# Norm table sent with x's first tile, five row chunks taken three steps at a time, weight copies inside DRAM begun earlier and at half the rate, sample sums ahead of the last store

## The chip, the cores and the metric

One core of a Trainium2 chip runs the kernel as one program. The metric is the device time of one execution in microseconds (us). The engines are TensorE (PE; its weight loads are listed apart as PEld), VectorE (DVE), ScalarE (ACT), GpSimd (POOL) and SyncE (SP). SP, ACT and POOL issue DMA transfers, all of which are carried by the core's 16 DMA engines.

## The reference

One step of a single decoder layer, in fp32, for 512 prompt tokens and 8 x 8 sample tokens (T = 576 columns in all), with a model width of 2048:

```
h  = rms_norm(x, norm_in)
z  = h @ w_in                      # all projections of both head groups at once
att = top-k sparse attention       # 8 heads of 128; an indexer (16 heads of 64) scores the keys, the best 256
                                   # (128 for the prompt) are kept; samples attend to 1024 paged keys as well
ob  = gated linear attention       # 4 heads, dk 128, dv 256, chunks of 64, a running state S
x  = x + concat(att * silu(ga), rms_norm(ob, gla_norm) * silu(gb)) @ w_out
y  = rms_norm(x, norm_f)           # 512 prompt rows and 64 sample rows
```

New keys, values, indexer keys and the states S are outputs too.

## The kernel before

**Numbers.** Every fp32 operand of a product is split in two rounded parts: a high part (`w_hi`, `xh`: a cast) and the rest (`w_lo`, `xl`: the operand less its high part). A product is then three matmuls, high by high, low by high and high by low. So each weight tile of 128x512 needs a load (`w_raw`, 256 KB, issued by SP), a cast on ACT and a subtraction on DVE, or on POOL during the first four heads (`lo_eng`). `wload` (L184) does these three.

**Stages.** The program is one long row of matmuls, with the work of the other engines laid beside it:
1. 0 to 26 us: `split_x(k)` loads x's 16 tiles of 128x576, multiplies each by its column of the table `gn_in` (norm_in) and splits it; `kmm` (L244) and `kmm_q` (L249) use each tile at once for the first two weight blocks, whose weights `first_piece` (L205) loads in pieces. For tile 0, x comes in two halves and the pieces of the first block are loaded by ACT's queue, as is `gn_in`.
2. to 130 us: the indexer's projections; to about 235 us: the queries and keys of heads 0 and 1, then `vgroup(0)`: values of four heads for all tokens. A value group has five accumulators (four chunks of 128 prompt rows, `ps_g`, and one for the samples, `ps_v`) and runs over 16 steps k, each with a weight of its own. Among its matmuls stand the sample indexer's products (`pq`, L507 and L508) of a page's keys (`kch`, `kcl`, L500 to L504).
3. to about 370 us: scores (`head_scores`, softmax at L732 to L739), gates (`head_g`) and outputs (`head_out`, transposes at L750) of heads 0 to 3, while DVE runs the top-k searches; to 640 us heads 4 to 7 with the samples' paged attention; `vgroup(1)` stands in head 4.
4. to 950 us: the gated linear attention (the state `Sst`, L1227). The value groups 2 and 3 belong to it.
5. to the end: the output product in seven block products (a form with sums of weight blocks), then a residual add, the final norm and the stores.

**Order.** A scheduler places each engine's instructions by estimated times; `tc.high_priority` moves what it holds ahead, `tc.issue_after(x)` puts an instruction behind x. Each engine then runs its own list in order. So an instruction that waits holds up everything behind it on its engine.

**Copies inside DRAM.** The sums of weight blocks for the output product are made by DMA alone: `block_parts` gives 16 parts of 512 KB. Each is first copied inside DRAM (`started`, issued by SP behind a weight load, L191) and later has a second block added to it by an accumulating DMA (`added`, issued by POOL behind a `w_lo`, L200). In the kernel before, the copies begin after `vgroup(0)`, one with each weight load, and the additions begin in head 2, one with each `w_lo` that POOL makes.

**End.** `store(c)` (L1440) scales the four quarters of 128 rows c by their root; of `store(1)`, quarter 3 is on DVE (L1447), quarters 0 and 2 on POOL (L1449), quarter 1 on ACT. The sample rows' last quarter comes from two products of 256 columns (`acc_s`); `sample_sum` adds the parts (L1354), `sample_square` (L1486) squares them, `mean_square`, `root_of` and a reciprocal give the factor, and L1581 to L1585 scale and store `y_smp`.

Of the kernel before, what the change touches and what calls it, by code (L numbers as in the profile page):

```python
# [20 lines left out]
P = 128  # L21
D = 2048
NK = D // P
# [96 lines left out]
def build(tc, I, O):  # L120
# [41 lines left out]

    gn_in = cp.tile([P, NK], F32, name="gn_in")
    eps = cp.tile([P, 1], F32, name="eps")
# [19 lines left out]
    def wload(src, far=0):  # L184
        with tc.high_priority(offset=WOFF):
            raw = wp.tile([P, 512], F32, name="w_raw", tag="w_raw", bufs=3)
            d = sy.dma_start(raw, src)
            wloads.append(d.ins if hasattr(d, "ins") else d)
            if started:
                with tc.issue_after(wloads[-1]):  # L190
                    sy.dma_start(*started.pop(0))  # L191
            hi = wp.tile([P, 512], F32R, name="w_hi", tag="w_hi", bufs=5)
            c = se.copy(hi, raw)  # L193
            rounded.append(getattr(c, "ins", c))
            lo = low_tile(wp, 5, far)
            c = lo_eng[0].tensor_tensor(out=lo, in0=raw, in1=hi.bitcast(F32), op=ALU.subtract)  # L196
# [4 lines left out]
        return hi, lo  # L201

    first_w = {}

# [13 lines left out]
    def split_x(k):  # L218
        xk = p0.tile([P, T], F32, name="xr", bufs=6)
        parts = (slice(HT, T), slice(0, HT)) if k == 0 else (slice(0, T),)  # L220
        for c in parts:
            sy.dma_start(xk[:, c], I["xT"][:, k, c])
        if k == 0:
            first_piece(0, k)
            se.dma_start(gn_in, I["norm_in"])
        if k % 2 == 0:
# [3 lines left out]
        l = xp.tile([P, T], F32R, name="xl", tag="xl")  # L230
        for c in parts:
            se.activation(h[:, c], xk[:, c], AF.Copy, scale=gn_in[:, k : k + 1])  # L232
        for c in parts:
            ve.scalar_tensor_tensor(out=l[:, c], in0=xk[:, c], scalar=gn_in[:, k : k + 1], in1=h[:, c].bitcast(F32), op0=ALU.mult, op1=ALU.subtract)
        xh.append(h)
# [408 lines left out]
    def vgroup(g, step):  # L644
# [19 lines left out]
        for k in range(NK):  # L664
# [106 lines left out]
    def head(h, bg, n):  # L771
# [194 lines left out]
    lo_eng[0] = ve  # L966
    assert not added
    with tc.issue_after(px["end"]):
# [227 lines left out]
    def recur(h, eL, qE, kDt, ks):  # L1196
# [17 lines left out]
        for i in range(4):  # L1214
# [10 lines left out]
            Sn = gl.tile([P, DV], F32, name="Sst", bufs=2)  # L1225
            if S is None:
                ve.tensor_copy(Sn, pU[:, :DV])  # L1227
            else:
                ve.scalar_tensor_tensor(out=Sn, in0=S, scalar=eL[:, i : i + 1], in1=pU[:, :DV], op0=ALU.mult, op1=ALU.add)
            S = Sn  # L1230
# [119 lines left out]
    y_smp = yp_.tile([P, D // 2], F32, name="y_smp")  # L1350
    nfs = yp_.tile([P, 256], F32, name="nfs")

# [56 lines left out]
    for c in range(2):  # L1409
        sy.dma_start(nfs[TS * c : TS * c + TS], I["norm_f"][:, 1024 * c + 768 : 1024 * c + 1024].to_broadcast([TS, 256]))  # L1410

# [27 lines left out]

    def store(c):  # L1440
        root_of(yr[:, c : c + 1], slice(0, P), c)
        ve.reciprocal(out=yr[:, c : c + 1], in_=yr[:, c : c + 1])
        done = {}
        for q in range(4):
            yc = place(c, q)
            if c > 1 or q == 3:
                done[ve] = ve.scalar_tensor_tensor(out=two(yc), in0=two(yc), scalar=yr[:, c : c + 1], in1=nfb(q), op0=ALU.mult, op1=ALU.mult)  # L1447
            elif q == 0 or (c == 1 and q == 2):
# [15 lines left out]

    def sample_sum(acc, q, c0, n, last=None):
        r, r2 = halves_of(q)
        d0 = 512 * q + c0
        yc = y_smp[r, d0 % 1024 : d0 % 1024 + n]
        t = ysm[q][:, c0 : c0 + n]
        if last is not None:  # L1470
            with behind(last, se):
                last[se] = se.copy(yl[r, c0 : c0 + n], acc[r2, :n])
            with behind(last, ve):
                plus(yc, acc[r, :n], t[r])
                last[ve] = plus(yc, yc, yl[r, c0 : c0 + n])
        else:
            plus(yc, acc[r, :n], t[r])
            plus(t[r], acc[r2, :n], t[r2])
            plus(yc, yc, t[r])

    def sample_square(q, c0, n, col):
        r, _ = halves_of(q)
        d0 = 512 * q + c0
        yc = y_smp[r, d0 % 1024 : d0 % 1024 + n]
        jk = ev.tile([P, 512], F32, name="yjk", tag="e1", bufs=2)
        se.activation(jk[r, :n], yc, AF.Square, accum_out=ysq[r, 4, col : col + 1])  # L1486

    def sample_weigh(q, c0, n):
        r, _ = halves_of(q)
        d0 = 512 * q + c0  # L1490
        for j in range(d0, d0 + n, 256):
            if j % 1024 < 768:
                yj = y_smp[r, j % 1024 : j % 1024 + 256]
                plus(yj, yj, a21[r, j // 256, :], ALU.mult)

    def sample_out(acc, q, c0, n, col):
        sample_sum(acc, q, c0, n)
        sample_square(q, c0, n, col)
        sample_weigh(q, c0, n)

# [23 lines left out]
    for p in range(2):  # L1524
# [12 lines left out]
        plus(y11[:, p], y11[:, p], acc)  # L1537
        sample_out(smp, q1, 0, 512, q1)
        for c in (0, 1):
# [4 lines left out]
    plus(y12[:, 0], y12[:, 0], acc)  # L1544
    sample_out(smp, 1, 0, 512, 1)
    for c in (0, 1):
# [3 lines left out]

    yl = ev.tile([P, T], F32, name="yl", tag="e0", bufs=2)[:, :512]
    r, r2 = halves_of(3)
    se.copy(yl[r], ysm[3][r2])
    plus(ysm[3][r], ysm[3][r], yl[r])
    accs = (pg.tile([P, 2, 512], F32, name="acc", tag="ps_g")[:, 0, :], pm.tile([P, 512], F32, name="acc_u", tag="pu", bufs=1))
    smp = [mm1("acc_s") for _ in range(2)]
    halves = (slice(0, 256), slice(256, 512))
    ws = [w for k in range(0, 8, 2) for w in weights("b22", 1, k)]
    for i in range(2):
# [3 lines left out]
        square(i, 3)  # L1563
        last = store(i)
    for s in range(2):
        with tc.issue_after(getattr(end, "ins", end)):
            for k in range(8):
                end = single(smp[s][:, :256], 8 + k, *(w[:, halves[s]] for w in ws[k]), k == 0, k == 7)
        sample_sum(smp[s], 3, 256 * s, 256, last)
        sample_square(3, 256 * s, 256, 3 + s)  # L1570
    with behind(last, ve):
        mean_square(pre[:, 4:5], ysq[:, 4:5, :4])
        ve.tensor_copy(pre[TS:, 5:6], pre[:TS, 4:5])
        last[ve] = ve.scalar_tensor_tensor(out=pre[TS:, 4:5], in0=pre[TS:, 4:5], scalar=-EPS, in1=pre[TS:, 5:6], op0=ALU.add, op1=ALU.add)
    with behind(last, ve):
        sample_weigh(3, 0, 256)
    root_of(yr[TS:, 5:6], slice(TS, P), 4)
    for r in (slice(0, TS), slice(TS, P)):
        ve.reciprocal(out=yr[r, 4:5], in_=yr[TS:, 5:6])
    a, b, c = y_smp[:, :448], y_smp[:, 448:768], y_smp[:, 768:]  # L1580
    se.activation(a, a, AF.Copy, scale=yr[:, 4:5])  # L1581
    se.dma_start(O["ys"][:, :448], a)
    ve.scalar_tensor_tensor(out=c, in0=c, scalar=yr[:, 4:5], in1=nfs, op0=ALU.mult, op1=ALU.mult)
    ve.tensor_scalar(out=b, in0=b, scalar1=yr[:, 4:5], scalar2=None, op0=ALU.mult)
    sy.dma_start(O["ys"][:, 448:], y_smp[:, 448:])  # L1585
    yp_s.close()
# [17 lines left out]
def host_inputs(a):  # L1604
# [4 lines left out]
    page = a["page_table"]  # L1609
    x = np.concatenate([xp, xs], 0)  # L1610
    ins = {
        "xT": c(x.reshape(T, NK, P).transpose(2, 1, 0)),
        "xp": c(xp),
# [50 lines left out]
```

## Time and profile before

| | |
|---|---|
| median of 3 runs | 1196.19 us (1195.59 to 1202.51) |
| the profiled execution's own time | 1196.95 us |
| its span (first to last recorded event) | 1194.9 us |
| PE busy | 1180.9 us, 99% of the span |
| DVE, ACT, POOL busy | 729.8, 585.9, 308.8 us |
| granted TensorE clock | 9 tenths or more in all 40 slices |
| bytes moved by DMA | 259.85 MB, 217 GB/s on average |

The profile is of one execution; 2.05 us of its time lie outside its span. Busy shares are averages over the stages above. Where PE is busy all the time, another engine's work shows in the time only if PE waits for it, or if it lies ahead of the first matmul or behind the last.

### The profile page before, as it was taken

The numbers are of one execution on the slowest core, as the hardware profiler recorded it, in microseconds if no ns is written. First come the engines' busy times: TensorE is split into PE (matmuls) and PEld (weight loads), VectorE is DVE, ScalarE is ACT, GpSimd is POOL, SyncE is SP. The second block draws the span as 40 slices with busy tenths as digits, with TensorE's granted clock in tenths as the row PEclk, the third lists the DMA queues.
The fourth block names the chain that finished last, engine by engine and source line by source line (L and its number), as shares of the span: only waits on it lengthen the run. The fifth ranks groups of instructions, "written<-read, shape, count | busy, mean of one in ns | idle before, by whom it ended". The sixth has DMA issues, their size and how long they took to land.

```text
span 1194.9 us, 23011 instructions
## 1 busy us (share of the span) xinstructions
PE 1180.9 (99%) x8389; PEld 1040.2 (87%) x8389; DVE 729.8 (61%) x1349; ACT 585.9 (49%) x1046; POOL 308.8 (26%) x495
## 2 busy tenths in 40 slices
PE   9999999999999999999999999999999999999997
PEld 8999997899999778889898769778899999888886
DVE  7678899699656433565453724434566444657686
ACT  6887565444443232354342635326367533544454
POOL 1225665546631110000110511321042121012101
PEclk9999999999999999999999999999999999999999
DMA  9562233877973999999667675677715377669873
GB/s 298 205 178 95 91 105 109 277 226 171 218 186 99 354 361 346 326 331 348 214 223 244 222 262 199 222 244 235 250 46 179 123 252 247 214 172 238 243 228 119
DMA packets 142563, 259.85 MB, mean 217 GB/s; under 512 B 15777, under 2 KB 39218, under 8 KB 141874
## 3 DMA queue, kind: packets, MB, share of 16 engines
q1 hardware_dynamic: 136370, 243.73, 60.9%
q0 software_dynamic: 4928, 13.11, 6.2%
q10 hardware_dynamic: 1152, 1.55, 0.4%
q8 instruction: 66, 1.08, 0.4%
q14 instruction: 47, 0.39, 0.1%
HBM read 224.49 MB, written 50.48 MB: 230 GB/s over the span
## 4 chain that ended last, share of the span: by engine, by line
PE 78%; DVE 9%; DMA 6%; issue 3%; ACT 2%; SPq 1%; POOL 0%; ACTq 0%; DVEq 0%; POOLq 0%
PE ps_g L244 35%; PE ps_g L249 6%; PE ps_g L658 4%; PE ps_g L657 4%; PE ps_g L659 4%; PE acc L1379 2%; PE acc L1380 2%; PE acc L1378 2%; PE pS L279 2%; PE pOs L279 2%; DMA y<-in_xp 2%; DVE w_lo L1373 1%; PE ps_v L653 1%; PE ps_v L654 1%; DVE wk L538 1%
## 5 line engine op out<-in xcount | busy, mean ns | idle before, releaser
L244 PE MATMUL ps_g<-xh,w_hi 128*128 128x288 f32 x1312 | 391.1, 298 | 0.8 <-ACT xh L232 0.8
L244 PE MATMUL ps_g<-xl,w_hi 128*128 128x288 f32 x1312 | 287.3, 296 | 0.1
L244 PE MATMUL ps_g<-xh,w_lo 128*128 128x288 f32 x1312 | 286.1, 296 | 0.0
L193 ACT CAST w_hi<-w_raw 128x512 fp32r<-128x512 f32 x252 | 154.4, 619 | 230.2 <-PE ps_g L244 84.0
L244 PEld LDWEIGHTS ps_g<-xh,w_hi 128*128 128x128 f32 x1312 | 246.4, 188 | 4.4 <-issue 1.7
L196 DVE TENSOR_TENSOR w_lo<-w_raw,w_hi 128x512 fp32r<-128x512 f32 x188 | 136.3, 729 | 173.9 <-ACT w_hi L193 167.8
L244 PEld LDWEIGHTS ps_g<-xl,w_hi 128*128 128x128 f32 x1312 | 211.9, 188 | 2.6 <-issue 1.2
L244 PEld LDWEIGHTS ps_g<-xh,w_lo 128*128 128x128 f32 x1312 | 211.8, 188 | 1.0
L657 PE MATMUL ps_g<-w_hi,xh 128*128 128x512 f32 x256 | 101.0, 396 | 0.9 <-DVE ev_t L617 0.9
L196 POOL TENSOR_TENSOR w_lo<-w_raw,w_hi 128x512 fp32r<-128x512 f32 x64 | 86.7, 1356 | 54.8 <-ACT w_hi L193 45.1
L659 PE MATMUL ps_g<-w_hi,xl 128*128 128x512 f32 x256 | 100.4, 392 | 0.0
L658 PE MATMUL ps_g<-w_lo,xh 128*128 128x512 f32 x256 | 100.3, 392 | 0.0
L1373 DVE TENSOR_TENSOR w_lo<-w_raw,w_hi 128x1024 fp32r<-128x1024 f32 (+1 forms) x60 | 68.4, 1150 | 41.8 <-ACT w_hi L1371 41.4
L1371 ACT CAST w_hi<-w_raw 128x1024 fp32r<-128x1024 f32 (+1 forms) x60 | 59.4, 995 | 61.5 <-PE acc_s L1383 21.1
L1379 PE MATMUL acc<-w_lo,fh 128*128 128x512 f32 x216 | 84.0, 389 | 0.0
L1380 PE MATMUL acc<-w_hi,fl 128*128 128x512 f32 x216 | 84.0, 389 | 0.0
L1378 PE MATMUL acc<-w_hi,fh 128*128 128x512 f32 x216 | 83.5, 389 | 0.0
L657 PEld LDWEIGHTS ps_g<-w_hi,xh 128*128 128x128 f32 x256 | 48.0, 188 | 11.2 <-DVE ev_t L617 1.3
L658 PEld LDWEIGHTS ps_g<-w_lo,xh 128*128 128x128 f32 x256 | 48.1, 188 | 10.5 <-issue 0.8
L659 PEld LDWEIGHTS ps_g<-w_hi,xl 128*128 128x128 f32 x256 | 48.1, 188 | 9.9
L668 POOL CAST xs<-xh 128x64 fp32r<-128x64 f32 x64 | 19.8, 309 | 119.5 <-PE ps_v L654 113.8
L618 POOL TENSOR_TENSOR ev_sw<-ev_sw,c_s 128x576 f32<-128x576 f32 x16 | 25.0, 1565 | 95.7 <-ACT ev_sw L615 95.6
(390 smaller groups left out, 2118.3 us busy)
## 6 DMA issues: line engine op xcount, KB each, us to landing
w_raw<-in_w SPq DMA_DIRECT2D x188, 256.0 KB, 3.6
kt<-in_ck SPq DMA_DIRECT2D x128, 256.0 KB, 5.2
vt<-in_cv SPq DMA_DIRECT2D x128, 256.0 KB, 5.2
w_raw<-in_wv SPq DMA_DIRECT2D x64, 256.0 KB, 3.2
w_raw<-st SPq DMA_DIRECT2D x32, 512.0 KB, 4.8
w_raw<-in_wo SPq DMA_DIRECT2D x20, 512.0 KB, 6.7
st<-in_wo SPq DMA_DIRECT2D x16, 512.0 KB, 4.7
bs<-in_wo SPq DMA_DIRECT2D x32, 256.0 KB, 5.3
```

The lines of the kernel that those rows point to most:

```text
L193: c = se.copy(hi, raw)
L196: c = lo_eng[0].tensor_tensor(out=lo, in0=raw, in1=hi.bitcast(F32), op=ALU.subtract)
L244: pe.matmul(ps[:, j, :HT], wt, xt[k][:, j * HT : (j + 1) * HT], start=(k == 0 and n in (0, 2)), stop=(k == NK - 1 and n > 3))
L249: m = pe.matmul(ps[:, 0, :TQ], wt[:, c], xt[:, P:T], start=(k == 0 and n == 0), stop=(k == NK - 1 and n == 2))
L657: pe.matmul(accs[i], xh[k][:, c], wh, start=a, stop=False)
L658: pe.matmul(accs[i], xh[k][:, c], wl, start=False, stop=False)
L659: m = pe.matmul(accs[i], xl[k][:, c], wh, start=False, stop=b)
L1371: se.copy(hi, raw)
L1373: ve.tensor_tensor(out=lo, in0=raw, in1=hi.bitcast(F32), op=ALU.subtract)
L1378: pe.matmul(acc, f[0][:, k, c], wh, start=a, stop=False)
L1379: pe.matmul(acc, f[0][:, k, c], wl, start=False, stop=False)
L1380: return pe.matmul(acc, f[1][:, k, c], wh, start=False, stop=b)
```

## The change

It has five parts.

1. The table `gn_in` becomes the first 16 columns of a tile `x0` that also holds x's tile 0. The first DMA brings the table and the first half (304 columns), the second the other half. ACT's DMA for the table is gone.
2. In `vgroup`, the first three steps k (before: the first two) are taken together, accumulator by accumulator.
3. The copies inside DRAM begin just before `vgroup(0)`, one with every second weight load; the additions begin in head 0, one with every second `w_lo` of POOL.
4. The update of the state `Sst` is placed under a priority (`ahead`).
5. At the end, the mean of the samples' first three quarters is made before the last products; the sums of the first 256 columns of the last quarter come before quarter 3 of `store(1)`; both halves of the last quarter are squared in one instruction of 512; the final scaling is 512 columns on ACT and 512 on DVE (with a table `nfs` of 512 columns that holds norm_f), in place of 448, 256 and 320.

```
-    gn_in = cp.tile([P, NK], F32, name="gn_in")
+    x0 = p0.tile([P, NK + T], F32, name="x0")
+    gn_in = x0[:, :NK]
...
-            if started:
+            if started and len(wloads) % 2:
                 with tc.issue_after(wloads[-1]):
                     sy.dma_start(*started.pop(0))
...
             if lo_eng[0] is po_:
-                if added:
+                turn[0] += 1
+                if added and turn[0] % 2:
                     with tc.issue_after(getattr(c, "ins", c)):
                         po_.dma_start(*added.pop(0), accum_op=ALU.add)
...
         if k == 0:
+            sy.dma_start(x0[:, : NK + HT], I["x0"][:, : NK + HT])
+            sy.dma_start(x0[:, NK + HT :], I["x0"][:, NK + HT :])
             first_piece(0, k)
-            se.dma_start(gn_in, I["norm_in"])
...
-            if k == 1:
+            if k == 2:
                 for i in (0, 1, 4, 2, 3):
-                    for kk in (0, 1):
+                    for kk in range(3):
                         mms(i, kk)
...
-            elif 1 < k < NK - 2:
+            elif 2 < k < NK - 2:
...
+            for to, src, _ in block_parts():
+                started.append((to, src))
             vgroup(0, lambda k: pump(bg, 2) if k % 4 == 3 else None)
...
-            for to, src, _ in block_parts():
-                started.append((to, src))
-        if h == 2:
-            assert not started
             for to, _, more in block_parts():
                 added.append((to, more))
...
+            with ahead():
+                if S is None:
+                    ve.tensor_copy(Sn, pU[:, :DV])
+                else:
+                    ve.scalar_tensor_tensor(out=Sn, in0=S, scalar=eL[:, i : i + 1], in1=pU[:, :DV], op0=ALU.mult, op1=ALU.add)
...
+    mean_square(pre[:, 4:5], ysq[:, 4:5, :3])
...
+        if s == 0:
+            plus(ys, a[r], t[r])
+            plus(t[r], a[r2], t[r2])
+            done[ve] = plus(ys, ys, t[r])
+            done = store(1, done)
+        else:
+            with behind(done, se):
+                se.copy(yl[r], a[r2])
+            with behind(done, ve):
+                plus(ys, a[r], t[r])
+                plus(ys, ys, yl[r])
+    jk = ev.tile([P, 512], F32, name="yjk", tag="e1", bufs=2)
+    se.activation(jk[r], y_smp[r, 512:], AF.Square, accum_out=ysq[r, 4, 4:5])
...
-    ve.scalar_tensor_tensor(out=c, in0=c, scalar=yr[:, 4:5], in1=nfs, op0=ALU.mult, op1=ALU.mult)
-    ve.tensor_scalar(out=b, in0=b, scalar1=yr[:, 4:5], scalar2=None, op0=ALU.mult)
-    sy.dma_start(O["ys"][:, 448:], y_smp[:, 448:])
+    ve.scalar_tensor_tensor(out=c, in0=c, scalar=yr[:, 4:5], in1=nfs, op0=ALU.mult, op1=ALU.mult)
+    sy.dma_start(O["ys"][:, 512:], c)
```

What the scheduler makes of it is read from each engine's list of instructions. First the start, on DVE, from its first cast on. `w_hi` and `w_lo` of 128x256 are pieces of the two first weight blocks, `xl` the low part of x's tile 0 in two halves. Before:

```order
L215 CAST w_hi<-w_raw 128x256
L216 TENSOR_TENSOR w_lo<-w_raw,w_hi 128x256
L234 SCALAR_TENSOR_TENSOR xl<-xr,gn_in,xh 128x288 x2
L215 CAST w_hi<-w_raw 128x256
L216 TENSOR_TENSOR w_lo<-w_raw,w_hi 128x256
```

After (the tile `x0` bears the name x_94 here):

```order
L218 CAST w_hi<-w_raw 128x256
L239 SCALAR_TENSOR_TENSOR xl<-x_94,xh 128x288
L219 TENSOR_TENSOR w_lo<-w_raw,w_hi 128x256
L218 CAST w_hi<-w_raw 128x256
L239 SCALAR_TENSOR_TENSOR xl<-x_94,xh 128x288
L219 TENSOR_TENSOR w_lo<-w_raw,w_hi 128x256
```

The first `w_lo` now stands behind the first `xl`, and `xl` waits for `xh` from ACT.

Second, PE where the last head projection ends and `vgroup(0)` begins, with the tiles' numbers: `pq_2322` and `pq_2441` are the products of two consecutive pages' keys, `ps_g` the row chunks. Before, from the first `pq` on, and then from the second:

```order
L507 MATMUL pq_2322<-kch_2256,qiS_603 128x512
L508 MATMUL pq_2322<-kcl_2259,qiS_603 128x512
L657 MATMUL ps_g_2392<-w_hi_2397,xh_125 128x512
L658 MATMUL ps_g_2392<-w_lo_2399,xh_125 128x512
L659 MATMUL ps_g_2392<-w_hi_2397,xl_126 128x512
...
L653 MATMUL ps_v_2394<-w_hi_2406,xs_2410 128x512
L654 MATMUL ps_v_2394<-w_lo_2408,xs_2410 128x512
L507 MATMUL pq_2441<-kch_2340,qiS_603 128x512
L508 MATMUL pq_2441<-kcl_2343,qiS_603 128x512
```

After, at the same place:

```order
L512 MATMUL pq_2320<-kch_2254,qiS_601 128x512
L513 MATMUL pq_2320<-kcl_2257,qiS_601 128x512
L512 MATMUL pq_2412<-kch_2338,qiS_601 128x512
L513 MATMUL pq_2412<-kcl_2341,qiS_601 128x512
L662 MATMUL ps_g_2390<-w_hi_2396,xh_123 128x512
L663 MATMUL ps_g_2390<-w_lo_2398,xh_123 128x512
L664 MATMUL ps_g_2390<-w_hi_2396,xl_124 128x512
L662 MATMUL ps_g_2390<-w_hi_2405,xh_140 128x512
L663 MATMUL ps_g_2390<-w_lo_2407,xh_140 128x512
L664 MATMUL ps_g_2390<-w_hi_2405,xl_141 128x512
L662 MATMUL ps_g_2390<-w_hi_2448,xh_161 128x512
```

The second page's product has moved 16 matmuls forward, directly behind the first, and the third step's weight is used by the seventh matmul of the group. In the value groups 1 and 2, PE's list has not changed at all, and in group 3 only at one place.

Third, DVE at the very end, from the last add of a row chunk's product (`acc_u`) on. Before:

```order
L1354 TENSOR_TENSOR y_12830<-y_12830,acc_u 128x512
L1442 RECIPROCAL yr<-yr 128x1
L1447 SCALAR_TENSOR_TENSOR y_12830<-y_12830,yr,e_12152 128x512
L1354 TENSOR_TENSOR y_smp<-acc_s,ysm_12836 64x256
L1354 TENSOR_TENSOR y_smp<-y_smp,yl 64x256
L1354 TENSOR_TENSOR y_smp<-acc_s,ysm_12836 64x256
L1354 TENSOR_TENSOR y_smp<-y_smp,yl 64x256
L1433 TENSOR_REDUCE pre<-ysq 128x1
L1434 TENSOR_SCALAR pre<-pre 128x1
L1573 COPY pre<-pre 64x1
L1574 SCALAR_TENSOR_TENSOR pre<-pre 64x1
L1354 TENSOR_TENSOR y_smp<-y_smp,e_12152 64x256
```

After, from the same add to the end of the list but its branch:

```order
L1358 TENSOR_TENSOR y_12828<-y_12828,acc_u 128x512
L1358 TENSOR_TENSOR y_smp<-acc_s,ysm_12834 64x256
L1358 TENSOR_TENSOR ysm_12834<-acc_s,ysm_12834 64x256
L1446 RECIPROCAL yr<-yr 128x1
L1358 TENSOR_TENSOR y_smp<-y_smp,ysm_12834 64x256
L1452 SCALAR_TENSOR_TENSOR y_12828<-y_12828,yr,e_12150 128x512
L1358 TENSOR_TENSOR y_smp<-acc_s,ysm_12834 64x256
L1358 TENSOR_TENSOR y_smp<-y_smp,yl 64x256
L1575 RECIPROCAL yr<-yr 64x1 x2
L1579 SCALAR_TENSOR_TENSOR y_smp<-y_smp,yr,nfs 128x512
```

The first half's three sums now stand on both sides of the reciprocal, ahead of quarter 3 of `store(1)`; the five small operations between the last sum and the last reciprocals have gone from this place.

Elsewhere: on SP copies inside DRAM now stand among the weights of `vgroup(0)` and its page loads, one behind every second weight. The rows of `Sst` on DVE stand where they stood.

More of the change, by code (lines that the diff above doesn't have):

```diff
@@ L201, in wload @@
         return hi, lo
+    turn = [0]
     first_w = {}
@@ L230, in split_x @@
         l = xp.tile([P, T], F32R, name="xl", tag="xl")
[L231 to L234, printed above, removed]
+        for c, x in parts:
+            se.activation(h[:, c], x, AF.Copy, scale=gn_in[:, k : k + 1])
+        for c, x in parts:
+            ve.scalar_tensor_tensor(out=l[:, c], in0=x, scalar=gn_in[:, k : k + 1], in1=h[:, c].bitcast(F32), op0=ALU.mult, op1=ALU.subtract)
         xh.append(h)
@@ L966, in build @@
     lo_eng[0] = ve
-    assert not added
+    assert not started and not added
     with tc.issue_after(px["end"]):
@@ L1350, in build @@
     y_smp = yp_.tile([P, D // 2], F32, name="y_smp")
[L1351 removed]
+    nfs = yp_.tile([P, 512], F32, name="nfs")
     def plus(out, a, b, op=ALU.add):
@@ L1445, in store @@
             yc = place(c, q)
-            if c > 1 or q == 3:
-                done[ve] = ve.scalar_tensor_tensor(out=two(yc), in0=two(yc), scalar=yr[:, c : c + 1], in1=nfb(q), op0=ALU.mult, op1=ALU.mult)
+            if q == 3 and gate:
+                with behind(gate, ve):
+                    done[ve] = ve.scalar_tensor_tensor(out=two(yc), in0=two(yc), scalar=yr[:, c : c + 1], in1=nfb(q), op0=ALU.mult, op1=ALU.mult)
+            elif c > 1 or q == 3:
+                ve.scalar_tensor_tensor(out=two(yc), in0=two(yc), scalar=yr[:, c : c + 1], in1=nfb(q), op0=ALU.mult, op1=ALU.mult)
             elif q == 0 or (c == 1 and q == 2):
@@ L1463, in behind, with sample_out @@
         return tc.issue_after(getattr(last[eng], "ins", last[eng]))
-    def sample_sum(acc, q, c0, n, last=None):
+    def sample_out(acc, q):
         r, r2 = halves_of(q)
[L1467 to L1484, printed above, removed]
-        jk = ev.tile([P, 512], F32, name="yjk", tag="e1", bufs=2)
[L1486 to L1499, printed above, removed]
+        d0 = 512 * (q % 2)
+        yc, t = y_smp[r, d0 : d0 + 512], ysm[q]
+        plus(yc, acc[r], t[r])
+        plus(t[r], acc[r2], t[r2])
+        plus(yc, yc, t[r])
+        jk = ev.tile([P, 512], F32, name="yjk", tag="e1", bufs=2)
+        se.activation(jk[r], yc, AF.Square, accum_out=ysq[r, 4, q : q + 1])
+        if q % 2 == 0:
+            for j in range(2):
+                yj = yc[:, 256 * j : 256 * j + 256]
+                plus(yj, yj, a21[r, 2 * q + j, :], ALU.mult)
     for p in range(2):
@@ L1563, in build @@
         square(i, 3)
[L1564 removed]
+        if i == 0:
+            store(0)
+    done = {}
     for s in range(2):
+        c = slice(256 * s, 256 * s + 256)
         with tc.issue_after(getattr(end, "ins", end)):
             for k in range(8):
[L1568 to L1576, printed above, removed]
+                end = single(smp[s][:, :256], 8 + k, *(w[:, c] for w in ws[k]), k == 0, k == 7)
+        ys, t, a = y_smp[r, 512 + 256 * s : 768 + 256 * s], ysm[3][:, c], smp[s][:, :256]
+        if s == 0:
[3 more added lines that the diff above has]
+            done = store(1, done)
+        else:
+            with behind(done, se):
[5 more added lines that the diff above has]
+    se.activation(jk[r], y_smp[r, 512:], AF.Square, accum_out=ysq[r, 4, 4:5])
     root_of(yr[TS:, 5:6], slice(TS, P), 4)
[L1578 to L1580 removed]
+    for h in (slice(0, TS), slice(TS, P)):
+        ve.reciprocal(out=yr[h, 4:5], in_=yr[TS:, 5:6])
+    a, c = y_smp[:, :512], y_smp[:, 512:]
     se.activation(a, a, AF.Copy, scale=yr[:, 4:5])
[L1582 removed]
+    se.dma_start(O["ys"][:, :512], a)
     ve.scalar_tensor_tensor(out=c, in0=c, scalar=yr[:, 4:5], in1=nfs, op0=ALU.mult, op1=ALU.mult)
[L1584 to L1585 removed]
+    sy.dma_start(O["ys"][:, 512:], c)
     yp_s.close()
```

35 lines of the change are left out of this document (17 added, 18 removed).

## The prediction

> **What bounds the kernel now.** I read the page first (busy shares), then the list of what PE waits for, and then the timeline at each place that the change touches.
>
> ```profile
> PE 1180.9 (99%) x8389; PEld 1040.2 (87%) x8389; DVE 729.8 (61%) x1349; ACT 585.9 (49%) x1046; POOL 308.8 (26%) x495
> ...
> PE ps_idle L286 <- DVE sst L379: 1.0, 1, 1.0
> PE pt L750 <- DVE p L739: 1.0, 2, 0.8
> PE ps_g L657 <- DVE ev_t L617: 0.9, 1, 0.9
> PE pS L276 <- DMA kt<-in_ck: 0.8, 1, 0.8
> PE ps_g L244 <- ACT xh L232: 0.8, 1, 0.8
> PE pO L1219 <- DVE Sst L1227: 0.5, 1, 0.5
> ```
>
> The columns are us in total, times, longest. PE is busy 99% of the span, and its named waits come to 5.0 us (a seventh, on the cast of a weight, is shorter still); the change takes no matmul away. So what it can win is small: parts of these waits, of the start (first real matmul at 5.76 us) and of the end (the last product's sums begin at 1186.95, the span ends at 1194.9). Even all of it would be 5.0 less the start's two rows (1.0 and 0.8), plus 5.8, plus 8.0, thus about 17 us, and most of that is transfer time that no edit touches. What it can lose is larger, where it makes PE wait anew.
>
> **Start (part 1).**
>
> ```profile
> 1.23 0.39 ACTq L225 DMA_DIRECT2D gn_in<-in_norm_in  x1
> ...
> 5.01 0.43 DVE L216 TENSOR_TENSOR w_lo<-w_raw,w_hi 128x256 fp32r<-128x256 f32 x1
> 5.18 0.96 ACT L232 ACTIVATE xh<-xr,gn_in 128x288 fp32r<-128x288 f32 x2 [2.52 <-DMA gn_in<-in_norm_in]
> 5.74 1.01 DVE L234 SCALAR_TENSOR_TENSOR xl<-xr,gn_in,xh 128x288 fp32r<-128x288 f32 x2 [0.31 <-ACT xh L232]
> 5.76 0.40 PE L244 MATMUL ps_g<-xh,w_hi 128*128 128x288 f32 x1 [0.80 <-ACT xh L232]
> 6.00 0.59 PE L244 MATMUL ps_g<-xh,w_lo 128*128 128x288 f32 x2
> ...
> 6.42 0.29 PE L244 MATMUL ps_g<-xh,w_hi 128*128 128x288 f32 x1
> 6.81 0.53 PE L244 MATMUL ps_g<-xl,w_hi 128*128 128x288 f32 x2
> ```
>
> ACT's first `xh` waits for the table, which was the third transfer to be asked for. Without it, `xh` can start when x's first half is there; ACT's row ends its wait at 5.18, and I put the landing of the enlarged first DMA at about 4.9 (an estimate: the first piece of weight, asked for at the same time, had landed and been cast before 5.01). Then `xh` is done at about 5.43 and PE starts at 5.48 instead of 5.76. But on DVE `w_lo` now stands behind `xl`, and `xl` behind `xh`: `xl` 5.47 to 6.05 (the two took 1.01, overlapped), `w_lo` 6.05 to 6.48 (0.43), and the second matmul comes at about 6.53 instead of 6.00, 0.53 later. In exchange the two `xl` matmuls no longer wait: between the rows at 6.42 and 6.81 lie 0.39 us for a matmul whose neighbours follow each other in 0.13, so 0.26 us comes back. Sum: **0.25 us later**. Behind this PE has slack on no other engine that would return it. From both sides: −0.3 (the whole 0.28 of the earlier `xh`, and no cost of `w_lo`) and +0.7 (0.53 and a little, without the 0.26).
>
> **The first value group (part 2, and the page product that moved).**
>
> ```profile
> 171.58 0.62 ACT L504 CAST kcl<-kcl 64x512 fp32r<-64x512 f32 x1 [0.81 <-DVE kcl L503]
> ...
> 172.92 1.30 POOL L196 TENSOR_TENSOR w_lo<-w_raw,w_hi 128x512 fp32r<-128x512 f32 x1 [1.93 <-DMA kc<-in_cidx]
> ...
> 177.74 0.39 PE L657 MATMUL ps_g<-w_hi,xh 128*128 128x512 f32 x1
> 178.20 0.75 DVE L617 TENSOR_TENSOR ev_t<-ps_g,c_c 128x576 f32<-128x576 f32 x1
> 179.00 0.50 PE L657 MATMUL ps_g<-w_hi,xh 128*128 128x512 f32 x1 [0.88 <-DVE ev_t L617]
> ```
>
> The second page's product now stands directly behind the first, at about 171.15. Its low keys `kcl` come from ACT at 171.58 + 0.62 = 172.20, so PE must wait about 0.9 to 1.1 us there, where before it had 16 matmuls to put in between. Behind it, all of the group queues. But the old wait at 177.74 to 179.00 (1.26 us for a matmul that takes 0.23 to the next, so 1.03 lost) hangs on DVE's `ev_t`, whose place in DVE's list is unchanged: the same 28 value-group matmuls stand ahead of it as before, and a PE that comes 0.9 to 1.1 us later finds it done or nearly. One wait replaces the other: **+0.1 us**. The third step's `w_lo` ends on POOL at 172.92 + 1.30 = 174.22; its first use moves up to about 174.3 with the new wait, so it is just in time. Bounds: −0.4 (if the page product's keys come earlier, the old wait remains at its floor, and only queue order wins a little) and +0.9 (both waits whole). For the other value groups PE's list stays as it is (group 3 has one swap), at nothing.
>
> **The transfers inside DRAM (part 3).** Before, the additions ran in heads 2 and 3, one with each weight:
>
> ```profile
> 290.00:310.00 20.00, 19.89 (x149) 19.52 (x149) 19.66 (x37) 6.97 (x11) 13.49 (x21) 1.00 1.00 223
> ...
> DMA to landing us min/median/max: 6.0/8.3/9.6
> ...
> DMA to landing us min/median/max: 2.5/7.8/12.2
> ...
> 313.60 0.62 ACT L193 CAST w_hi<-w_raw 128x512 fp32r<-128x512 f32 x1 [1.62 <-DMA w_raw<-in_w]
> ...
> 317.82 0.16 DVE L738 RECIPROCAL mx<-mx 128x1 f32<-128x1 f32 x1 [1.50 <-ACT p L736]
> ...
> 317.70 0.29 PE L244 MATMUL ps_g<-xh,w_hi 128*128 128x288 f32 x1
> 318.77 0.33 PE L750 MATMUL pt<-c_ident,p 128*128 128x128 f32 x1 [0.77 <-DVE p L739]
> ```
>
> In the row by stage the last two numbers are the DMA share (1.00 from 290 to 310) and GB/s; the two landing rows are those of the additions (L200, all 16, issued from 281 to 338 us) and of the weight loads (L187) of 281 to 340 us. The chain reads: with an addition for each weight the 16 DMA engines are full, a weight takes up to 12.2 us to land, ACT's cast waits for it with the softmax exponential behind it in ACT's list, so DVE's `p` and then the transposes come late. PE loses 1.07 − 0.13 = 0.93 us here, and by the same sum 0.37 at 315.2: 1.3 in all. At half the rate an addition has two weights' time, and the share falls to about half between 281 and 338 us and rises before. A weight's median landing was 3.0 us in the first value group, without such transfers. So both waits should go: **−1.3 us**. What is late next is the paged keys' `kt` (0.8 in the list of waits); its loads are released in head 3, whose end moves with PE, so the gain is kept. Bounds: −1.6 (with 0.27 us at 304.4, where PE waits for `kl`, which took 1.77 us beside a POOL subtraction) and +0.8 (the additions now stretch over heads 0 to 3 and make one such wait elsewhere). The copies themselves now lie in the first value group, at half their rate; I hold them hidden. DMA was busy 0.36 there (190 to 210 us; the first landing row is that of the weights of 171 to 230 us). And where a copy went with each weight (243 to 270 us, the second landing row), weights still landed in 2.6 us in the median.
>
> ```profile
> 190.00:210.00 20.00, 20.00 (x90) 16.57 (x89) 19.16 (x43) 11.47 (x21) 12.39 (x19) 1.00 0.36 103
> ...
> DMA to landing us min/median/max: 2.5/3.0/4.3
> ...
> DMA to landing us min/median/max: 2.5/2.6/5.4
> ```
>
> **Part 4** moves nothing in any engine's list near `Sst`: 0, and its wait of 0.5 stays. That part does not do what it says.
>
> **The end (part 5).**
>
> ```profile
> 1185.80 0.75 DVE L1447 SCALAR_TENSOR_TENSOR y<-y,yr,e 128x512 f32<-128x512 f32 x1
> ...
> 1186.95 0.43 DVE L1354 TENSOR_TENSOR y_smp<-acc_s,ysm 64x256 f32<-64x256 f32 x1 [0.40 <-ACT yl L1472]
> ...
> 1187.99 1.55 POOL L1449 TENSOR_SCALAR y<-y,yr 128x512 f32<-128x512 f32 x1
> ...
> 1188.21 0.73 DVE L1354 TENSOR_TENSOR y_smp<-y_smp,yl 64x256 f32<-64x256 f32 x1
> ...
> 1189.79 0.29 ACT L1438 ACTIVATE yr<-ysq,pre 64x1 f32<-64x1 f32 x1 [0.30 <-DVE pre L1574]
> 1190.11 0.33 DVE L1579 RECIPROCAL yr<-yr 64x1 f32<-64x1 f32 x2
> ...
> 1191.29 0.33 SPq L1585 DMA_DIRECT2D out_ys<-y_smp  x1
> ```
>
> Before, all four sums (1186.95 to 1188.94) come behind the last matmul; now two do, after quarter 3 of `store(1)`. That instruction moves behind the first half's sums, to about 1186.2, and lasts to 1186.95, so the two sums run 1187.05 to 1187.87 (0.43 and 0.42). Then a square of 512 (0.63 by the row at 1184.52 below, and I allow 0.2 to read the sum) to 1188.7, the root (0.29) and the reciprocals (0.33) to 1189.3, the last scaling at 512 columns (0.75 as at 1185.80) to 1190.1, and the store is issued at 1190.13, not 1191.29: −1.16. The five small operations of 1188.98 to 1189.7 are out of the way. Against it stand POOL's two scalings for `store(1)`, the second from 1187.99 on, beside which the sum at 1188.21 took 0.73 instead of 0.42; with a few such (0.3 to 0.4 each) about 0.5 is left. I take **−0.7 us**, between −1.2 and +0.4.
>
> ```profile
> 1184.52 0.63 ACT L1426 ACTIVATE yjk<-y 128x512 f32<-128x512 f32 x1 [0.44 <-DVE y L1354]
> 1187.41 0.42 DVE L1354 TENSOR_TENSOR y_smp<-y_smp,yl 64x256 f32<-64x256 f32 x1
> 302.94 1.77 DVE L626 TENSOR_TENSOR kl<-ev_t,kh 128x512 fp32r<-128x512 f32 x1
> ```
>
> The Trainium skill speaks against this part (SBUF — State Buffer, section Who interferes with whom): a VectorE instruction with two SBUF inputs and a GpSimd instruction that reads SBUF exclude each other, and whichever comes second blocks for the whole of the first. The trace agrees at 302.94, where `kl` took 1.77 us beside a POOL subtraction. It does not at 1187.41, where both inputs of the sum are in SBUF and it took 0.42 us beside POOL's first scaling, which ended only at 1187.99.
>
> **Sum:** 0.25 + 0.1 − 1.3 + 0 − 0.7 = −1.65 us against the profiled execution's own 1196.95 (span 1194.9 and 2.05 around it): 1195.3. The median of the runs shown, 1196.19, is 0.76 lower, so I forecast **1194.5 us**. About 1% (12 us) is what a measurement of this kernel can tell from no change, so this is no change.
>
> **Rivals.**
> - *The heads keep their waits*: the additions are as many as before, and a pair of them on top of a weight load is enough to delay a cast. For it: 6 to 9.6 us until an addition lands is longer than a weight's turn. Against it: the share of 1.00 needs one addition per weight. Then 1.3 us is missing: 1195.8.
> - *The end is held by POOL*: quarter 3 of `store(1)` waits behind POOL's first scaling (1.55 us as the second, from 1186.2 to about 1187.75), runs to 1188.5, and the last sum waits behind POOL's second, to 1190.05; the store is issued at about 1192.7, 1.4 later than before, not 0.7 earlier: 1196.6. For it the row at 302.94, against it those at 1187.41 and 1188.21. It is what the Trainium skill's rule above would give.
> - *Slower: the copies delay the first value group.* Each copy stands on SP directly behind a weight and ahead of the page loads and the next weight. The nearest case is the landing median of 7.8 us beside the additions: 4.8 more than 3.0, against a lead of `w_lo` over its matmul that I find to be 3.0 us at least (pairing the 16 steps). It decides when a weight lands over 3 us later than now. Then 1.8 us each time the three `w_raw` buffers turn over, for three turns that hold a copy in the way 5.4 us: about 1200. Against it: the share of 0.36, and 2.6 us of median landing with copies at the double rate.
> - *All goes well*: `w_lo` costs nothing at the start (−0.3), the end gives 1.2, the heads 1.6: 0.55 + 0.5 + 0.3 better, thus 1193.1.
>
> **How the numbers follow.** Chances: forecast 0.55 (own range 1192.8 to 1195.8), heads keep their waits 0.15, end held by POOL 0.10, copies delay 0.11, all well 0.09. The range runs from 1191.6 (all well, with the group's −0.4 and as much again for the runs' scatter) to 1199.0 (the POOL case with the start's and the group's worst, 1.3 more, and part of the copies' case). Faster by over 1% would need 12 us of the 17 above: 0.01. Slower by over 1% needs the copies' case twice over: 0.02. Within 1%: 0.97.
>
> **What would show it.** Right: the first real matmul near 5.5 and the second near 6.5; a wait of about 1 us on `kcl` at 171.4 and none on `ev_t`; no wait of `pt` on `p`; weight landings under 5 us from 281 to 340; the last store issued near 1190.1 to 1190.6. Wrong: PE waits in the list that name `w_hi`, `w_lo` or `kcl` between 171 and 235 us, or waits above 1 us in heads 0 and 1, where the additions are new.

## The result, and the profile after

The changed kernel takes **1204.88 us** (median of 15 runs, 1202.2 to 1207.3), the kernel before 1197.02 (15 runs, 1194.13 to 1202.51). The ratio is 1.0063, with a 95% interval of 1.0049 to 1.0077: 7.9 us slower. The forecast was 1194.5, within 1191.6 to 1199.0. The profiled execution took 1206.91 us, with a span of 1204.8; it is 2.0 us above the median, so that its span is 9.9 us longer than that of the profile before.

The page and the list of PE's waits, of the changed kernel (us in total, times, longest):

```profile
PE 1188.7 (99%) x8384; PEld 1043.0 (87%) x8389; DVE 728.1 (60%) x1347; ACT 584.7 (49%) x1043; POOL 308.3 (26%) x495
...
PEclk9999999989999999999999999999999999999998
...
PE pt L755 <- DVE mx L740: 2.7, 2, 1.9
PE pt L755 <- DVE p L744: 1.6, 2, 1.4
PE ps_idle L291 <- DVE sst L384: 1.0, 1, 1.0
PE ps_g L249 <- DVE w_lo L219: 0.6, 1, 0.6
PE pq L734 <- DVE kl L631: 0.5, 1, 0.5
PE pq L513 <- ACT kcl L509: 0.4, 1, 0.4
```

PE's list has as many matmuls as before (8389, of which the profile of the changed kernel lacks five) and yet PE is busy 7.8 us longer (1188.7 against 1180.9), though its share is still 99%. So most of the loss is not in waits at all. The waits of the transposes (`pt`) have grown from 1.0 to 4.3 us. Two slices of the granted clock show an 8: that of 241 to 271 us, and the last, which holds the end, where hardly any matmul is left (the last 10 us have 0.68, and 0.70 in the kernel before). With the matmuls of both lists paired, the changed kernel leads by 0.85 us at 28.9 us of the kernel before, by 2.2 at 112 and by 1.3 at 228, where the first value group ends; at 327 it is 5.9 us behind. From there the lag grows in steps: 6.6 at 640, 8.2 at 810, behind the value groups 2 and 3, 8.4 at 1000, and 9.9 at 1173, behind most of the output product. From the start of the last matmul to the end of the span both take 8.5 us.

The first place is head 0's softmax. The stage's windows (PE busy and count, then the other engines, the granted clock, DMA share, GB/s), of the changed kernel and of the kernel before:

```profile
245.00:250.00 5.00, 2.82 (x20) 2.35 (x19) 4.51 (x12) 4.03 (x10) 2.59 (x4) 0.97 0.23 71
250.00:255.00 5.00, 3.92 (x17) 3.91 (x18) 5.00 (x13) 3.19 (x5) 2.98 (x5) 0.50 1.02 239
255.00:260.00 5.00, 5.00 (x35) 5.00 (x35) 4.84 (x11) 1.31 (x3) 2.28 (x6) 0.85 0.96 220
260.00:265.00 5.00, 5.00 (x39) 4.78 (x38) 4.56 (x11) 1.98 (x4) 2.55 (x5) 1.00 0.88 225
```

```profile
235.00:255.00 20.00, 20.00 (x167) 18.84 (x160) 15.70 (x43) 10.24 (x19) 7.93 (x12) 1.00 0.79 247
```

The clock of a row is a mean over its stretch. PE is idle for 2.2 us of the first five and 1.1 of the next, and the clock's mean is 0.97, then 0.50 and 0.85. Shorter windows give 1.00 from 249.2 to 249.7, 0.50 from 249.8 to 256.5 and 1.00 from 256.6 on: one stretch of about 6.8 us at half the clock. It costs about as much again as the waits: 0.03, 0.50 and 0.15 of 5 us each are 3.4 us. The timeline of the changed kernel shows what the waits are for:

```profile
238.73 0.38 SPq L707 DMA_DIRECT2D v<-sv  x1
...
244.40 0.62 ACT L711 CAST vh<-v 128x512 fp32r<-128x512 f32 x1 [8.45 <-DMA v<-sv]
...
246.33 0.40 ACT L741 ACTIVATE p<-p,mx 128x128 f32<-128x128 f32 x1
...
245.05 0.69 DVE L712 TENSOR_TENSOR vl<-v,vh 128x512 fp32r<-128x512 f32 x1 [4.77 <-ACT vh L711]
...
249.32 1.54 POOL L197 TENSOR_TENSOR w_lo<-w_raw,w_hi 128x512 fp32r<-128x512 f32 x1
...
249.50 1.52 DVE L744 TENSOR_SCALAR p<-p,mx 128x256 f32<-128x256 f32 x1
...
248.98 0.33 PE L755 MATMUL pt<-c_ident,p 128*128 128x128 f32 x1 [1.88 <-DVE mx L740]
251.07 0.48 PE L755 MATMUL pt<-c_ident,p 128*128 128x128 f32 x1 [1.37 <-DVE p L744]
```

`vgroup(0)` stores its values in DRAM (`sv`), and head 0 reads its part back (`v`, in `head_v`). The read can begin only when the stores have landed. ACT casts `v` ahead of the exponentials (L741), and DVE makes its low part ahead of the rest of the softmax; so both lists stand for `v`, ACT for 8.45 us. In the kernel before, the same cast came at 241.58 after an idle time of 4.38, and that wait cost PE nothing:

```profile
241.58 0.62 ACT L706 CAST vh<-v 128x512 fp32r<-128x512 f32 x1 [4.38 <-DMA v<-sv]
```

The DMA issues of 222 to 246 us tell why it is late: of the changed kernel, and then of the kernel before (KB each, median us to landing):

```profile
w_raw<-in_w SPq DMA_DIRECT2D x5, 256.0 KB, 7.9
st<-in_wo POOLq DMA_DIRECT2D x2, 512.0 KB, 9.1
sv<-v_tok SPq DMA_DIRECT2D x4, 256.0 KB, 7.9
```

```profile
sv<-v_tok SPq DMA_DIRECT2D x4, 256.0 KB, 5.0
```

Two additions, which the kernel before does not issue until head 2, lie beside the stores, and a store takes 7.9 us instead of 5.0 in the median.

The second place is everywhere: PE's pace. In the same 120 us of the output product, where PE waits for nothing and the clock is 1.00, the changed kernel starts fewer matmuls; the rows are of the kernel before and of the changed one.

```profile
1040.00:1160.00 120.00, 120.00 (x531) 99.40 (x530) 78.93 (x74) 59.27 (x71) 17.59 (x20) 1.00 0.78 216
```

```profile
1040.00:1160.00 120.00, 120.00 (x526) 98.47 (x525) 78.23 (x66) 58.41 (x67) 17.61 (x20) 1.00 0.79 214
```

### The profile page after: what moved, and what is told of

Same layout as the page of the kernel before. It is cut to its first block, busy times and chain, and to the rows that moved or that the text cites. A ratio compares the mean times of both kernels' runs of the same rounds, so it can differ in the third digit from the quotient of the medians.

```text
span 1204.8 us, 22993 instructions
## 1 busy us (share of the span) xinstructions
PE 1188.7 (99%) x8384; PEld 1043.0 (87%) x8389; DVE 728.1 (60%) x1347; ACT 584.7 (49%) x1043; POOL 308.3 (26%) x495
## 4 chain that ended last, share of the span: by engine, by line
PE 91%; DVE 4%; DMA 2%; issue 1%; ACT 1%; POOL 0%; ACTq 0%; DVEq 0%; SPq 0%
PE ps_g L249 39%; PE ps_g L254 6%; PE ps_g L662 5%; PE ps_g L664 5%; PE ps_g L663 5%; PE acc L1382 4%; PE acc L1384 4%; PE acc L1383 4%; PE pOs L284 2%; PE pS L284 2%; PE ps_v L658 1%; PE ps_v L659 1%; PE acc_s L1388 1%; PE acc_s L1387 1%; DVE wk L543 1%; DVE top L540 1%
```

## The experiments

"Before" is the kernel before, run beside each (medians 1196.68, 1196.82, 1195.47 and 1196.87 in four batches). Times of different batches are compared below by their medians; the medians of the kernel before, the 1197.02 above among them, differ by up to 1.6 us, so such a difference is no surer than that.

**Part 3 undone** in the changed kernel.

```
-            if started and len(wloads) % 2:
+            if started:
...
-                if added and turn[0] % 2:
+                if added:
...                                  # block_parts: started after vgroup(0), added in head 2
```

> The changed kernel with its part 3 undone: copies begin after the first value group, one per weight, additions begin in head 2, one per weight, as before; parts 1, 2, 4 and 5 stay. Theory (the additions and copies of part 3 fill the DMA engines while the first value group's values are stored and read back, v comes late, and ACT and DVE hold the softmax of head 0 behind v): the waits of 2.0 and 1.5 us at 247 to 251 and the lowered clock of 235 to 270 (0.87, 0.95) go, the waits of head 2 (1.3 us) come back; time 1196 to 1198, at or just under the kernel before. Rival (the loss comes from the other parts, or from a slower pace of PE that part 3 has nothing to do with): 1201 to 1205.

Measured: 1200.16 us, ratio 1.0022 (1.0005 to 1.0040). The waits of head 0 and the low clock are gone (20.00 of 20 us busy from 235 to 255, clock 1.00); 4.7 of the 7.9 us come back. But it is still 3.5 us slower than the kernel before, between the two theories: something else costs. The two waits of head 2, which were to come back, did not; PE waits 0.8 us at 344 instead.

**Part 3 alone** in the kernel before (the same lines the other way round).

> The kernel before with part 3 alone. Theory: the whole loss is here, 1203 to 1206, with PE waits of over 1 us on p or mx in head 0 and a granted clock under 0.95 behind them. Rival (it needs part 2's other order of the value group, or the loss is elsewhere): 1196 to 1199, no such wait.

Measured: 1201.84 us, ratio 1.0038 (1.0020 to 1.0055), 5.2 us slower than its kernel before. That is between theory and rival again: the whole loss is not here. Head 0 looks as in the changed kernel, where PE is busy for 16.75 of these 20 us and the clock's mean is 0.87:

```profile
235.00:255.00 20.00, 17.01 (x126) 16.21 (x126) 13.72 (x38) 8.54 (x16) 7.62 (x12) 0.91 0.81 235
...
1040.00:1160.00 120.00, 120.00 (x531) 99.34 (x531) 78.54 (x71) 59.66 (x73) 17.62 (x20) 1.00 0.75 206
```

So part 3 brings the waits (2.5 us on `mx`, 1.4 on `p`) and the lower clock without part 2's help, and it does not bring the slower pace (531 matmuls, as before). The clock is at 0.50 for 3.4 us here, half as long as in the changed kernel.

**Copies early, additions late.**

```
                                     # in head(h), added is filled when h == 2
-                if added and turn[0] % 2:
+                if added:
```

> The changed kernel, but the additions begin in head 2 with every weight of POOL, as before; the copies stay early, one per second weight. Theory A (the additions in head 0 do it: three of them, 5.8 to 9.4 us to landing each, lie on the DMA engines when the values are stored, 217 to 240 us): v lands by about 240, no wait above 0.5 us in head 0, the two waits of head 2 (0.4 and 0.9) are back; 1196 to 1198. Theory B (the copies do it, which then still stand among the value stores): waits of 2 us or more in head 0 remain and the time is 1202 or more.

Measured: 1199.47 us, ratio 1.0015 (0.9997 to 1.0034). The stores of the values land after 2.7 us in the median, and the cast comes 7.6 us earlier than in the changed kernel:

```profile
sv<-v_tok SPq DMA_DIRECT2D x4, 256.0 KB, 2.7
...
236.81 0.62 ACT L710 CAST vh<-v 128x512 fp32r<-128x512 f32 x1 [1.72 <-DMA v<-sv]
...
235.00:255.00 20.00, 20.00 (x164) 19.68 (x163) 18.41 (x49) 10.16 (x19) 9.75 (x14) 1.00 0.51 156
```

Theory A holds: it is the additions in head 0. The copies among the first values' weights, the slower rival of the prediction, cost nothing that shows; 5.0 us, with the copies at the old rate, is even longer than 2.7. The time missed its expectation by 1.5 us, the same remainder as above. Of the two waits of head 2, one of 0.5 us came back.

**The same transfers, head 0's values cast behind the softmax.**

```
+        with tc.issue_after(px["exp"]) if h == 0 else ExitStack():
             se.copy(vh, v32)
             ve.tensor_tensor(out=vl, in0=v32, in1=vh.bitcast(F32), op=ALU.subtract)
```

> The changed kernel with the same transfers, but in head 0 the cast of the values (ACT) and their low part (DVE) are put behind the last exponential, so that the softmax no longer stands behind them in either list. Theory (the loss is the in-order list behind v, and the clock that is lowered after the wait): v still lands at about 244, the exponentials start at about 240 instead of 246, the waits on mx and p in head 0 fall from 3.5 to under 1 us, the clock stays at 1.00; 1198 to 1200. Rival (late weights themselves, landing 8 to 9 us after issue, hold PE): the waits stay, named w_hi or w_lo, and the time stays at 1203 or more.

Measured: 1200.86 us, ratio 1.0029 (1.0010 to 1.0048). The stores still take 7.4 us in the median and the DMA engines are full, and PE is busy throughout:

```profile
239.52 0.40 ACT L742 ACTIVATE p<-p,mx 128x128 f32<-128x128 f32 x1 [2.48 <-DVE mx L741]
...
245.11 0.60 ACT L712 CAST vh<-v 128x512 fp32r<-128x512 f32 x1
...
235.00:255.00 20.00, 20.00 (x164) 19.54 (x163) 18.58 (x48) 10.46 (x19) 10.17 (x16) 1.00 1.03 281
```

So full DMA engines alone do not cost PE anything in head 0; it is what stands behind the late transfer in ACT's and DVE's lists. At 303 to 306 us PE now waits 1.1 us for `kh` and 0.7 for `kl`. The time is 0.9 us above the expected range, and again some 4 us remain.

**Where the tiles lie.** Paired by stage, the pace was the same in all kernels with parts 1, 2, 4 and 5, and another in the kernel before and in part 3 alone. Part 1 takes a tile of 64 bytes a partition from the left side of SBUF, and everything above it, the weights `w_hi` and `w_lo`, the head tiles and the output product's forms, moves down by 64 bytes, while x's parts `xh` and `xl`, on the right side, stay; so do the output product's own weights, but for those of its first product (`n=1`), which lie on the left. The next kernels move these tiles by an idle tile and change nothing else: the lists of PE, DVE, ACT and SP are the same word for word.

```
+    pad = cp.tile([P, NK], F32, name="pad")      # 64 bytes; 2 * NK: 128, NK // 2: 32
+    po_.memset(pad, 0.0)
```

In the changed kernel, back to the old addresses:

> The changed kernel with an idle tile of 16 columns (64 bytes a partition, set to zero once by POOL) where the table gn_in stood in the kernel before. It does nothing but put the weights, the forms of the output product and the head tiles back at the addresses that they had before; they lie 64 bytes lower in the changed kernel. Theory (the address sets PE's pace: a 512-column matmul follows the last in 228.9 to 233 ns in the changed kernel and in 226.7 to 227.5 before, in every stage alike in kernels without the table's move): the pace of the output product is 226.7 ns again, and 3 to 4 us come back, 1200.5 to 1202; the waits in head 0 and the lowered clock stay. Rival (the pace is the clock's, or that of other parts of the change): 229 ns and 1204 to 1206.

Measured: 1201.99 us, ratio 1.0044 (1.0028 to 1.0059): 2.9 us less than the changed kernel, with its waits of head 0 and 531 matmuls in the window again. In the kernel before, 64 bytes up:

> The kernel before with the same idle tile of 64 bytes beside its table, so that the same tiles lie 64 bytes higher and nothing else changes. Theory (address): the pace is that of the changed kernel, 229 ns in the output product, about 233 in the value groups, 200 in place of 205 for the 448-column matmuls of the start; 3 to 4 us slower than before, 1199.5 to 1201, with the same waits as before. Rival (pace by another cause): 1195.5 to 1197.5.

Measured: 1204.42 us, ratio 1.0068 (1.0048 to 1.0088), 7.6 us slower: twice what was expected, with the direction right. The paces, 233, 230 and 202 ns where 229, 233 and 200 were expected, are not those of the changed kernel, since the same tiles have moved the other way. And by 128 and by 32 bytes:

> The kernel before with an idle tile of 128 bytes a partition beside its table: the same tiles lie 128 bytes higher, at the same remainder by 128 as before (64). Theory (the pace hangs on where the operands lie within 128 bytes): 226.7 ns in the output product, 1195.5 to 1197.5, as before. Rival (any move of the tiles changes the pace, or a longer period counts): a pace of 228 ns or more and 1199 or more.

Measured: 1204.82 us, ratio 1.0058 (1.0035 to 1.0081). My theory of a period of 128 bytes falls, and the rival stands.

> The kernel before with an idle tile of 32 bytes a partition: the tiles on that side lie at 96 by 128, x's parts stay at 64. Theory: the pace of the 512-column matmuls lies between that of the kernel before (227) and that of the 64-byte move (231 to 233), or at the latter; no faster than before: 1196 to 1204. Rival (only the sum of the two operands' remainders, or a 64-byte line, counts): at or below 226.7 ns, 1194 to 1197.

Measured: 1207.65 us, ratio 1.0081 (1.0056 to 1.0105), above both ranges. The window of the output product, of the moves by 64, 128 and 32 bytes:

```profile
1040.00:1160.00 120.00, 120.00 (x516) 96.19 (x515) 76.41 (x69) 57.68 (x70) 17.58 (x20) 1.00 0.75 206
```

```profile
1040.00:1160.00 120.00, 120.00 (x516) 96.56 (x515) 77.15 (x67) 58.44 (x71) 17.59 (x20) 1.00 0.74 205
```

```profile
1040.00:1160.00 120.00, 120.00 (x516) 96.59 (x516) 77.65 (x65) 59.00 (x69) 17.58 (x20) 1.00 0.74 203
```

The addresses are those of the built programs; no trace shows them. A matmul has a moving operand, whose columns run through PE, and a stationary one, which the weight load puts there. With the moving operand's address less the stationary one's, by 256, and the mean step from one matmul's start to the next of the same kind (steps over 267 ns at 512 columns and 233 ns at 448, which are waits, left out), one order fits all that have 512 columns:

```
difference by 256     512 columns, output product   512 columns, value groups   448 columns
  0  (before, pad)    226.7 ns                      227.7 ns                    204.6 ns
 64                   228.9 (changed)               230.2 (64 up)               200.3 (changed)
192                   233.3 (64 up)                 233.2 (changed)             202.3 (64 up)
128                   233.7 (128 up)                232.5 (128 up)              203.9 (128 up)
 32 or 224            233.2 (32 up)                 233.2 (32 up)               204.0 (32 up)
```

In the kernel before, the operands of these matmuls lie at the same remainder, 192, which is the fastest for 512 columns and the slowest for 448. The changed kernel mixes 64 (output product, and the 448-column matmuls of the start, which it makes faster by 4 ns) with 192 (value groups). The output product's row is without its first 48 matmuls: there both operands lie on the left side and move together, and the step is 227.0 to 227.6 ns in every one of these kernels, so what counts is where the two lie to each other. The 288-column matmuls of the heads move least, from 131.9 ns to 132.1 in the changed kernel and 132.7 with the move by 64 bytes, but some 3600 such steps make about 1 and 3 us; the expectation for the move had left these out. That the addresses set the pace is shown; why they do is not.

**Both causes taken away**: the idle tile with late additions, and the idle tile with the late cast.

> The changed kernel with the idle tile and with the additions in head 2, one per weight (copies early at half rate). Theory (two causes, which add: additions and copies among the first values, and the address): neither is left, so the gains of the start and the end show: 1194.5 to 1196.5, below the kernel before by up to 2. Rival (the parts do not add, something else costs): 1197.5 or more.

Measured: 1196.65 us, ratio 0.9997 (0.9984 to 1.0010).

> The changed kernel with the idle tile and with the cast of head 0's values behind the last exponential; all transfers as in the changed kernel. Theory: 1196 to 1198 (the address gives 3 to 4 of the 1200.9 without the tile). Rival: 1199 or more.

Measured: 1196.74 us, ratio 0.9998 (0.9988 to 1.0008). The parts add: 2.8 and 4.1 us less than the same kernels without the tile (2.2 and 3.7 by the ratios, each to the kernel before of its own batch), and level with the kernel before. The expected gain of up to 2 us is not there.

**What is left, tried for a version below both.** The first with late additions, the second with part 3 undone, both with the idle tile and with x's low part behind the first `w_lo`:

```
+            with tc.issue_after(low) if k == 0 else ExitStack():
                 ve.scalar_tensor_tensor(out=l[:, c], in0=x, ...)     # low: first_piece's subtraction
```

> The changed kernel with the idle tile, the additions in head 2 with every weight, and at the start x's low part put behind the first w_lo on DVE (the order of the kernel before; the table stays with x's first tile). Theory (the second matmul waits 0.5 us for w_lo behind xl): the second matmul comes near 5.1 us instead of 5.6, and 0.3 to 0.5 us are kept to the end: 0.3 to 0.5 below the version with the idle tile and late additions (1196.65), about 1196.2, not told apart by the times but by the trace. Rival: the gain is taken back at once by the xl matmuls, which then wait.

Measured: 1195.68 us, ratio 0.9992 (0.9977 to 1.0008). The second matmul comes at 5.29 us, where the version with the idle tile and late additions has it at 5.62, but the `xl` matmuls come at 6.50 instead of 6.32: the lead is gone at once, as the rival said.

> The changed kernel with the idle tile, part 3 undone (copies after the first value group, additions in head 2, one per weight) and the same order at the start: what parts 1, 2 and 5 are worth at the old addresses. Theory: 1195.0 to 1196.5, the start 0.9 to 1.2 us earlier than in the kernel before, the tail within 0.5 of it, nothing else gained. Rival (part 2 or 5 costs something of its own): 1197 or more.

Measured: 1197.10 us, ratio 1.0009 (0.9993 to 1.0024). That is the rival's range, 0.6 us above the theory's, but the interval holds no change: parts 1, 2 and 5 together are worth nothing that can be measured, and whether one of them costs a little stays open. None of these versions beats the kernel before clearly.

## Why the prediction was wrong

**Start** (forecast 0.25 us later): 0.45 us earlier at the matmul that follows the first ones (8.32 before, 7.86 after). The step that failed is the landing.

```profile
4.09 0.29 DVE L218 CAST w_hi<-w_raw 128x256 fp32r<-128x256 f32 x1 [3.09 <-DMA w_raw<-in_w]
4.28 0.53 ACT L237 ACTIVATE xh<-x 128x288 fp32r<-128x288 f32 x1 [1.61 <-DMA x<-in_x]
...
5.82 0.53 PE L249 MATMUL ps_g<-xh,w_lo 128*128 128x288 f32 x2 [0.55 <-DVE w_lo L219]
```

The cost of `w_lo` behind `xl` is as forecast (0.55 us, the wait in the last row). But x's half was there by 4.28, not 4.9; the first weight, too, came 0.6 us earlier, which no run explains.

**First value group** (+0.1): right in kind, and in part by luck. The wait on `ev_t` is gone from the list, and one on `kcl` is there, but of 0.4 us and at another page's product, at 193 us; at the one forecast, of 0.9 to 1.1 us, it is there only when part 3 is undone (0.8).

**The transfers** (−1.3, at most +0.8): here the sign was wrong. Part 3 costs 4.7 us (undone) to 5.2 us (alone). I read the additions through weight loads alone, and weights did land sooner from 281 to 340 us, in 3.3 us in the median instead of 7.8. The step that failed is "the additions now stretch over heads 0 to 3 and make one such wait elsewhere": I did not look for what else crosses DRAM in head 0. It is the values' store and read back, a chain of two transfers with ACT's and DVE's lists behind it, and I priced it at one wait, without the lowered clock, which cost as much again. Waits above 1 us in heads 0 and 1 were named as a sign of being wrong, but with no price in the sum. The slower rival named the wrong transfers, the copies, which cost nothing. Of the two waits in head 2, the one on `p` at 315 to 319 us did not go either; it came back as 0.8 us on `mx` at 322.

**`Sst`** (0): right; its rows did not move.

**The end** (−0.7): 0.0. From the last matmul's start to the end of the span it is 8.5 us in both. The first half's sums come ahead of quarter 3 as forecast, but beside POOL's two scalings quarter 3 of `store(1)` and the last sum take longer:

```profile
1195.91 3.34 POOL L1456 TENSOR_SCALAR y<-y,yr 128x512 f32<-128x512 f32 x2 [39.92 <-DVE yr L1446]
...
1196.29 1.07 DVE L1452 SCALAR_TENSOR_TENSOR y<-y,yr,e 128x512 f32<-128x512 f32 x1
...
1197.86 0.81 DVE L1358 TENSOR_TENSOR y_smp<-y_smp,yl 64x256 f32<-64x256 f32 x1
1198.70 0.63 ACT L1572 ACTIVATE yjk<-y_smp 64x512 f32<-64x512 f32 x1 [1.72 <-DVE y_smp L1358]
```

1.07 instead of 0.75 and 0.81 instead of 0.42 are 0.7 us; no run takes POOL's scalings away, so that they are the cause is not shown. The last store is issued 4.6 us behind the last matmul's start, 0.3 earlier than the 4.9 before, where the forecast's own times had 1.16; the first 512 columns, now 256 KB by ACT's queue, then land after 2.8 us, where the last store before took 2.6. The rule of the Trainium skill (SBUF — State Buffer, section Who interferes with whom) points the right way, but neither instruction was held to the end of the scaling beside it (POOL's first lasts to 1197.70, its second to 1199.26); its rival, +1.4, did not come.

**The missing term**: the addresses, 2.8 to 4.1 us by the medians (less by the ratios: 1.6 to 3.7). This is the second step that failed: the prediction held PE's pace fixed, from "the change takes no matmul away". With part 3's 4.7 to 5.2 and the rest near nothing, the sum is 7.5 to 9.3 by the medians, about the 7.9 us measured.

**The range**: its lower end does not follow from its terms (1193.1 less the group's 0.5 and as much again is 1192.1, not 1191.6), and nothing hangs on it. The 1% that the prediction takes for the least that can be told apart is too coarse: the interval of the ratio is 0.14% to either side, so 7.9 us are a change, if a small one.

## What to carry to other kernels

Before transfers are moved into a stage, list every transfer of that stage that someone waits for, spills and their reads first, and see what stands behind that wait on each engine's list. A table taken out of a pool moves all tiles above it: compare the operands' addresses of the costly matmuls before and after, and keep them with an idle tile if the matmul count per window falls. Where PE is 99% busy, a longer busy time with the same matmuls is the first thing to look at.

## What the runs showed of the hardware

- The step from one 512-column fp32r matmul to the next was 226.7 to 233.7 ns, by where its two operands lie to each other by 256 bytes; at equal remainders 512 columns were fastest (226.7) and 448 columns slowest (204.6, against 200.3 at 64 apart). Where both operands moved together, the step stayed at 227.0 to 227.6 ns. Over this kernel a move of 32 to 128 bytes cost 7.6 to 10.8 us.
- A wait of PE of 1.9 us was enough to halve the granted clock: it ended at 248.98, and the clock fell at 249.7, as the second wait of 1.4 us began, and stayed at 0.50 for 6.8 us. With the idle tile in the changed kernel it fell at 249.2, between a wait of 1.8 and one of 1.1, for 6.8 us again; with part 3 alone it fell at 250.8, behind waits of 1.6 and 1.4, for 3.4 us. Single waits of 1.2 us in the other runs left it at 1.00. The Trainium skill (TensorE: Matmul & The Clock Gate, section What's actually happening) gives an idle window of about 3.4 us for it; here no single wait was that long.
- Beside a POOL subtraction of a weight (249.32 to 250.86), DVE's scaling of `p` of 256 columns took 1.52 us, and ended 0.2 us behind it; that of 384 columns, at 252.35, took 0.40. PE's second wait of head 0 ends with it.
